# One V projection by halves of the tokens, two steps ahead of the gate transposes, and four row sums by matmul against ones

## The chip, the cores and the metric

The kernel runs on one core of a Trainium2 chip. The metric is the device time of one execution in microseconds; the median of three runs stands for a kernel. TensorE (PE, with its weight loads PEld), VectorE (DVE), ScalarE (ACT), GpSimd (POOL) and SyncE (SP, which issues almost all DMA transfers) each work through their own list of instructions in order, and wait for one another by semaphores.

## The reference

The reference is one decoder layer for 512 tokens of width 1024, in float32. The parts that matter here:

```python
mods = (silu(c) @ w_ada + b_ada).reshape(B, 9, 1, 1024)
sh1, sc1, gt1, sh2, sc2, gt2, sh3, sc3, gt3 = [mods[:, i] for i in range(9)]
h = rmsnorm(x, g_pre[0]) * (1 + sc1) + sh1
x = x + 0.5 * gt1 * rmsnorm(swiglu(h, w_gu1, w_dn1), g_post[0])      # first FFN
h = rmsnorm(x, g_pre[1]) * (1 + sc2) + sh2
y = token_mixer(h, ...)                        # z = h @ w_in, linear attention + softmax attention
x = x + gt2 * rmsnorm(y, g_post[1])
...                                            # second FFN, like the first
```

`swiglu` is 1024 to 2 x 2816, silu(g) * u, and back to 1024 through `w_dn`. In the mixer the softmax attention has 16 heads; its v is 1024 columns of `h @ w_in`, and its forget gates are 16 columns whose logarithms are summed along the tokens.

## The kernel before

Every float32 operand of a large matmul is split into a high part (fp32r) and a rest, and a product takes three matmuls (`mm3`, L203). A weight block of 128 x 1024 values is loaded by SP into one of four `raw` tiles (L151), copied to `whi` by ACT (L166), and `wlo = raw - whi` is made by DVE (L167). There are five `whi` and five `wlo` tiles. A `raw` tile is free for the next load when DVE has made its `wlo`.

The first FFN ends with `down`: two halves of the output columns (`dh`), and in each half 11 groups of two k-blocks of `w_dn` (the last three of the second half are taken together); a group is 24 matmuls, four token tiles with six each. The FFN's matmuls before that (L394 for the ordinary blocks) end with block `jb = 10`, whose results DVE multiplies (L523) and splits (L210).

Between the groups of the first half the modulation columns of the layer are made. `ada_acc` (L222, L224) loads `w_ada` in four pieces into `raw` tiles and sums, on DVE, eight rows weighted by silu(c) into one tile of 128 x 512. What is still to be summed over the 128 partitions is done on PE. For the gates (`mod_gate`) that tile is split in two (`two_parts`: ACT L209, DVE L210) and PE multiplies it with a tile of ones (L307, L308). For shift and scale of the second sub-layer (`mod_cols`, four calls, one for each 256 columns) `mod_reduce` makes four matmuls with one column of ones (L279), and `mod_turn` (L286 to L288) adds biases on DVE. The first call stands at `jb = 10`, the other three in `down`, each with its loads and sums ahead of a group and its matmuls (`rest`) behind the next one.

After `down`, `make_h` normalises and transposes x for token tiles 0 and 1, then 2 and 3 (L343, L353, L367), and the mixer begins. `Fill` is a list of steps, each with a load and a run; loads go up to four steps ahead of runs. `F.nat` adds the eight steps of one V projection: for each of four pairs of k-blocks (`kb`), first token tiles 0 and 1 (`tp = 0`), then 2 and 3. The forget gates come after the first V projection: a matmul (L787), a chain on DVE and ACT, a scan (L840), and four small transposes (L847), which wait for the scan. The steps of the second V projection are called after these in the program. The order of instructions on each engine is set by a scheduler when the kernel is built, and is fixed from then on; where several things are ready by its reckoning it does not keep to the order in which the code names them.

Of the kernel before, what the change touches and what calls it, by code (L numbers as in the profile page):

```python
# [13 lines left out]
ALU = mybir.AluOpType  # L14

P = 128
# [7 lines left out]
QA, KA, VA, AL, RA, QB, KB, VB, FB, GA, GB = (  # L24
    0, 512, 1024, 2048, 2064, 3088, 4112, 5136, 6160, 6176, 7200)
# [15 lines left out]
def tile_hybrid_layer(  # L41
# [4 lines left out]
    nc = tc.nc  # L46
# [12 lines left out]
    def nm(s):  # L59
        uid[0] += 1  # L60
        return f"{s}_{uid[0]}"

    def unit(dt=F32, shape=(P, 512)):
        return sb.tile(list(shape), dt, tag="u", bufs=NU, name=nm("u"))

    def tmp(shape=(P, 512), dt=F32):
        return sb.tile(list(shape), dt, tag="t2", bufs=NTMP, name=nm("t2"))
# [4 lines left out]
    def acc(shape=(P, 512)):  # L72
        return pm.tile(list(shape), F32, tag="mm", name=nm("mm"))

    def aux(shape=(P, 512)):
        return pa.tile(list(shape), F32, tag="aux", name=nm("aux"))

    def small(n, tag="sm", bufs=16):
        return sb.tile([P, n], F32, tag=tag, bufs=bufs, name=nm(tag))
# [25 lines left out]
    ident = sb.tile([P, P], F32, tag="ident", name="ident")  # L105
    make_identity(nc, ident)
    ones_r = sb.tile([P, P], F32R, tag="ones", name="ones")
# [93 lines left out]
    def mm3(ps, a, b, first, last):  # L201
        for n, (i, j) in enumerate(PARTS):
            nc.tensor.matmul(ps, a[i], b[j], start=first and n == 0, stop=last and n == 2)  # L203

    def cut(pair, cs):
        return pair[0][:, cs], pair[1][:, cs]

    def hilo(hi, lo, src, eng=None):
        nc.scalar.copy(hi, src)  # L209
        (eng or nc.vector).tensor_tensor(lo, src, hi.bitcast(F32), ALU.subtract)  # L210


    def ada_acc(src):

        a = tmp()
        for kh in range(4):
            raw = sb.tile([P, 2, 512], F32, tag="raw", bufs=NRAW, name=nm("raw"))
            src(raw, kh)
            for j in range(2):
                k = kh * 2 + j  # L220
                if k == 0:
                    nc.vector.tensor_scalar(a, raw[:, j, :], csil[:, 0:1], None, ALU.mult)  # L222
                else:
                    nc.vector.scalar_tensor_tensor(a, raw[:, j, :], csil[:, k:k + 1], a, ALU.mult, ALU.add)  # L224
        return a

    def two_parts(a):
        pair = unit(F32R), unit(F32R)
        hilo(*pair, a)
        return pair  # L230
# [18 lines left out]
    def ada_sum_b(us, k0):  # L249

        a = tmp()
        nc.vector.tensor_scalar(a, us[k0], csil[:, k0:k0 + 1], None, ALU.mult)
        for k in range(k0 + 1, KD):
            nc.vector.scalar_tensor_tensor(a, us[k], csil[:, k:k + 1], a, ALU.mult, ALU.add)
        nc.vector.tensor_tensor(a, a, us[0], ALU.add)
        return a

    def col_pair():
        return (sb.tile([P, KD], F32, tag="shc", bufs=2, name=nm("shc")),
                sb.tile([P, KD], F32, tag="scc", bufs=2, name=nm("scc")))  # L260

    def mod_cols(shc, scc, i, ch):

        w2 = w_ada[:, 3 * i * D:(3 * i + 2) * D].rearrange("(k p) (m c) -> p k m c", p=P, m=2)

        def src(raw, kh):
            for m in range(2):
                nc.sync.dma_start(raw[:, :, m * 256:(m + 1) * 256],
                                  w2[:, 2 * kh:2 * kh + 2, m, ch * 256:(ch + 1) * 256])
        a = ada_acc(src)  # L270

        def rest():
            mod_turn(shc, scc, i, ch, mod_reduce(a))
        return rest

    def mod_reduce(a):
        ps = aux((P, 4))
        for j in range(4):
            nc.tensor.matmul(ps[:, j:j + 1], a[:, j * P:(j + 1) * P], ones[:, 0:1], start=True, stop=True)  # L279
        return ps  # L280

    def mod_turn(shc, scc, i, ch, ps):
        js = slice(2 * ch, 2 * ch + 2)
        b0 = 24 * i + 2 * ch
        g0 = 72 + 8 * i + 2 * ch
        nc.vector.scalar_tensor_tensor(scc[:, js], ps[:, 2:4], 1.0, cols[:, b0 + 8:b0 + 10], ALU.add, ALU.add)  # L286
        nc.vector.tensor_tensor(shc[:, js], ps[:, 0:2], cols[:, b0:b0 + 2], ALU.add)
        nc.vector.tensor_tensor(scc[:, js], scc[:, js], cols[:, g0:g0 + 2], ALU.mult)  # L288
# [282 lines left out]
    with in_order(last):  # L571
# [51 lines left out]
        a = ada_sum_b(ada[0], ROWS_A[0])  # L623
# [3 lines left out]
        for ch in range(4):  # L627
            ks, part = (2 * ch, 2 * ch + 1), 3 if ch < 3 else 4
            gu_matmuls(ps0, *first, hs, ks, slice(0, 512), range(part), True)
            if ch < 3:  # L630
                a = ada_sum_b(ada[ch + 1], ROWS_A[ch + 1])
# [3 lines left out]
                modulated(ch + 1, a, (5, 4, 0)[ch])  # L635
            gu_matmuls(ps0, *first, hs, ks, slice(0, 512), range(part, 4), True)
    sh2, sc2 = col_pair()
    extra = [lambda ch=ch: mod_cols(sh2, sc2, 1, ch) for ch in range(4)]
    nxt = []

    def after1(t):
# [12 lines left out]

    sh3, sc3 = col_pair()
    extra = [lambda ch=ch: mod_cols(sh3, sc3, 2, ch) for ch in range(4)]

    halves = (slice(0, 64), slice(64, P))

    class Fill:  # L660
# [23 lines left out]
            late = []  # L684
            self.add(lambda: late.append(fn()), lambda: late[0]())

        def nat(self, c0, evac):

            blk = Block(w_in, 0, KD, c0, 512)
            ps = []  # L690

            def step(kb, tp):
                if not ps:
                    ps.extend(acc() for _ in range(NT))
                for t in (2 * tp, 2 * tp + 1):
                    for k in (2 * kb, 2 * kb + 1):
                        mm3(ps[t], cut(hs[k], slice(t * P, (t + 1) * P)), blk[k], k == 0, k == KD - 1)
                    if kb == 3:
                        evac(t, ps[t])
            for kb in range(4):  # L700
                for tp in range(2):
                    self.add(lambda kb=kb, tp=tp: None if tp else blk.load(2 * kb, 2 * kb + 2),
                             lambda kb=kb, tp=tp: step(kb, tp))

        def tr(self, todo, evac):

# [58 lines left out]
    F = Fill()  # L765
# [2 lines left out]

    vb = [[unit(), unit()] for _ in range(NT)]
    for g in range(2):  # L770
        F.nat(VB + g * 512, lambda t, ps, g=g: nc.scalar.copy(vb[t][g], ps))
    fqk = []
    F.qk_parts(QB, KB, 0.125, fqk)
    F.until(8)
# [67 lines left out]
            0.0 if i == 0 else Fr[f_, i * P - 1:i * P], ALU.mult, ALU.add)  # L842
    Fd = dr.tile([16, T], F32, name="Fd")
    nc.sync.dma_start(Fd, Fr[f_])
    ftp = aux((P, 4, 16))
    for i in range(NT):
        nc.tensor.transpose(ftp[:, i, :], Fr[f_, i * P:(i + 1) * P], ident[f_, f_])  # L847
# [167 lines left out]
    for h in range(4):  # L1015
        zp = acc()
        nc.tensor.matmul(zp, wa2[0:80, h * P:(h + 1) * P], alow[0:80], start=True, stop=True)
        u = unit()
# [272 lines left out]
```

## Time and profile before

| | |
|---|---|
| median of three runs | 1421.57 us (1421.54 to 1423.88) |
| the profiled execution | 1425.45 us, span of the profile 1423.4 us |
| PE busy | 1361.4 us, 96% of the span |
| DVE, ACT, POOL busy | 910.4, 595.5, 206.6 us |
| mean granted TensorE clock | 0.992 |

All times in the rows are microseconds from the start of the span. The profiled execution is 2.05 us longer than its span, and 3.9 us longer than the median of the three runs. PE busy counts pipelined matmuls whose ends are modelled; the step from one start to the next is the better price of a matmul.

### The profile page before, as it was taken

Reading aid. Unit: us, or ns where it says so; the run is one execution under the profiler, and the core shown is the slowest. Engines: PE = TensorE matmul, PEld = TensorE weight load, DVE = VectorE, ACT = ScalarE, POOL = GpSimd, SP = SyncE. Lnnn points to the kernel's source line nnn. Section 1 sums busy time; section 2 is a strip of 40 time slices with the busy share of each in tenths; the row PEclk is TensorE's granted clock in tenths of the full one; section 3 lists DMA queues with packets and bytes.
Section 4 is the critical chain, followed back from the end, with each engine's and each line's share of the span. In section 5 each row is a group of like instructions: output and inputs, shape, how many; then the busy total and the mean of one; then the engine's idle time right before and its main releaser. Section 6 shows DMA issues by size and latency. Waiting matters only on the chain.

```text
span 1423.4 us, 19497 instructions
## 1 busy us (share of the span) xinstructions
PE 1361.4 (96%) x7485; PEld 1146.4 (81%) x7485; DVE 910.4 (64%) x1410; ACT 595.5 (42%) x1026; POOL 206.6 (15%) x328
## 2 busy tenths in 40 slices
PE   4899999999999999999999999999999999999998
PEld 3699899888877867777888887787878999987886
DVE  6888678685266689762745546538577877866222
ACT  6444444223154476663723333332355444433221
POOL 6200000000050644340110202100050000000001
PEclk8999999999999999999999999999999999999999
DMA  9413233597336755322232232125631332346431
GB/s 322 150 62 112 82 104 110 179 290 265 103 107 182 226 163 167 94 71 78 90 117 75 60 87 62 60 74 160 210 119 45 119 119 75 104 134 196 130 118 59
DMA packets 164089, 180.84 MB, mean 127 GB/s; under 512 B 9226, under 2 KB 128118, under 8 KB 163996
## 3 DMA queue, kind: packets, MB, share of 16 engines
q1 hardware_dynamic: 163564, 178.81, 40.2%
q8 instruction: 59, 0.97, 0.3%
q10 hardware_dynamic: 432, 0.79, 0.2%
q14 instruction: 34, 0.28, 0.1%
HBM read 173.25 MB, written 6.32 MB: 126 GB/s over the span
## 4 chain that ended last, share of the span: by engine, by line
PE 71%; DVE 15%; DMA 6%; ACT 3%; issue 3%; POOL 2%; SPq 0%; DVEq 0%; POOLq 0%; ACTq 0%
PE mm L203 47%; PE mm L394 11%; PE mm L456 7%; DVE wlo L167 5%; DMA raw<-in_w_gu_dram 3%; PE aux L1108 1%; DMA u<-in_w_ada_dram 1%; DVE u L210 1%; DVE t L473 1%; ACT whi L166 1%; DMA raw<-in_w_ada_dram 1%; PE aux L919 1%; PE mm L930 1%; DVE u L907 1%; DVE raw L444 1%
## 5 line engine op out<-in xcount | busy, mean ns | idle before, releaser
L166 ACT CAST whi<-raw 128x1024 fp32r<-128x1024 f32 x262 | 273.3, 1050 | 516.7 <-PE mm L203 261.8
L167 DVE TENSOR_TENSOR wlo<-raw,whi 128x1024 fp32r<-128x1024 f32 x260 | 323.1, 1248 | 247.6 <-ACT whi L166 244.1
L203 PE MATMUL mm<-whi,u 128*128 128x512 f32 x1216 | 392.1, 398 | 1.7 <-DVE t L367 1.5
L203 PE MATMUL mm<-u,whi 128*128 128x512 f32 x896 | 289.9, 402 | 0.8 <-DVE u L1135 0.8
L456 PE MATMUL mm<-u,whi 128*128 128x256 f32 x1568 | 279.3, 281 | 10.6 <-DVE t L473 10.6
L203 PEld LDWEIGHTS mm<-whi,u 128*128 128x128 f32 x1216 | 228.2, 188 | 54.9 <-ACT u L209 1.7
L456 PEld LDWEIGHTS mm<-u,whi 128*128 128x128 f32 x1568 | 239.8, 188 | 13.9 <-DVE t L473 13.2
L203 PE MATMUL mm<-wlo,u 128*128 128x512 f32 x608 | 240.3, 395 | 1.0 <-DVE wlo L167 1.0
L456 PE MATMUL mm<-u,wlo 128*128 128x256 f32 x784 | 219.0, 280 | 0.0
L203 PEld LDWEIGHTS mm<-u,whi 128*128 128x128 f32 x896 | 167.3, 189 | 39.3 <-DVE u L1135 1.2
L394 PE MATMUL mm<-u,whi 128*128 128x512 f32 (+1 forms) x576 | 168.5, 380 | 11.0 <-ACT u L209 9.9
L203 PE MATMUL mm<-u,wlo 128*128 128x512 f32 x448 | 178.6, 399 | 0.0
L456 PEld LDWEIGHTS mm<-u,wlo 128*128 128x128 f32 x784 | 147.3, 188 | 0.0
L203 PEld LDWEIGHTS mm<-wlo,u 128*128 128x128 f32 x608 | 114.2, 188 | 28.8 <-DVE wlo L167 1.3
L394 PEld LDWEIGHTS mm<-u,whi 128*128 128x128 f32 x576 | 105.4, 191 | 35.1 <-ACT u L209 13.2
L394 PE MATMUL mm<-u,wlo 128*128 128x512 f32 (+1 forms) x288 | 105.4, 375 | 0.0
L203 PEld LDWEIGHTS mm<-u,wlo 128*128 128x128 f32 x448 | 84.7, 189 | 19.7
L321 POOL TENSOR_SCALAR sm<-ss 128x1 f32<-128x1 f32 x12 | 2.3, 190 | 642.9 <-ACT jk L328 642.9
L224 DVE SCALAR_TENSOR_TENSOR t<-raw,csil,t 128x512 f32<-128x512 f32 x98 | 74.0, 756 | 10.0 <-DMA raw<-in_w_ada_dram 7.8
L394 PEld LDWEIGHTS mm<-u,wlo 128*128 128x128 f32 x288 | 55.3, 192 | 10.3
L209 ACT CAST u<-t 128x256 fp32r<-128x256 f32 (+1 forms) x94 | 40.8, 454 | 43.5 <-DVE t L523 23.0
L876 POOL TENSOR_SCALAR u<-t,Ft 128x128 f32<-128x128 f32 (+1 forms) x64 | 44.3, 702 | 90.5 <-DMA t<-Fd 67.1
(197 smaller groups left out, 1381.1 us busy)
## 6 DMA issues: line engine op xcount, KB each, us to landing
raw<-in_w_gu_dram SPq DMA_DIRECT2D x88, 512.0 KB, 3.9
raw<-in_w_in_dram SPq DMA_DIRECT2D x64, 512.0 KB, 3.8
raw<-in_w_dn_dram SPq DMA_DIRECT2D x44, 512.0 KB, 5.2
raw<-in_w_ada_dram SPq DMA_DIRECT2D x64, 256.0 KB, 3.7
raw<-in_w_ada_dram SPq DMA_DIRECT2D x24, 512.0 KB, 5.2
u<-in_w_ada_dram SPq DMA_DIRECT2D x32, 256.0 KB, 6.3
raw<-in_w_in_dram SPq DMA_DIRECT2D x20, 256.0 KB, 2.8
t<-Fd SPq DMA_DIRECT2D x16, 256.0 KB, 5.1
```

The source lines that it names most:

```text
L166: nc.scalar.copy(hi, raw)
L167: (eng or nc.vector).tensor_tensor(lo, raw, hi.bitcast(F32), ALU.subtract)
L203: nc.tensor.matmul(ps, a[i], b[j], start=first and n == 0, stop=last and n == 2)
L209: nc.scalar.copy(hi, src)
L210: (eng or nc.vector).tensor_tensor(lo, src, hi.bitcast(F32), ALU.subtract)
L224: nc.vector.scalar_tensor_tensor(a, raw[:, j, :], csil[:, k:k + 1], a, ALU.mult, ALU.add)
L394: nc.tensor.matmul(p_[:, ts], w_[k][i][:, cs], hs[k][e][:, ts], start=ks[0] == 0 and n == 0, stop=ks[-1] == KD - 1 and n == 3 * len(ks) - 1)
L444: nc.vector.tensor_tensor(a12, a12, a11, ALU.subtract)
L456: nc.tensor.matmul(ps[:, j], *((h_[:, js], w_) if self.turned else (w_[:, js], h_)), start=first and k + j + m == 0, stop=k == 3 and m == ...
L473: nc.vector.tensor_tensor(o, ps, a, ALU.add)
L876: nc.gpsimd.tensor_scalar(s_at(s, i), fb[:, 0:n], -1.0, Ft[:, i, h:h + 1], ALU.mult, ALU.add)
L907: nc.vector.tensor_scalar(s_at(S[e], i), s_at(S[e], i), rs[e][:, i:i + 1], None, ALU.mult)
```

## The change

`mod_cols` gets a second form (`as_row`), used for the four calls of the second sub-layer: the sum tile is split in two right after it is made, PE multiplies both parts with the tile of ones (two matmuls of 128 x 512 in place of the four with one column), and DVE takes the needed column from each 128 x 128 piece by a multiplication with the identity and a sum along the row (`tensor_tensor_reduce`, four of them). The first V projection takes all four `kb` for `tp = 0` and then all four for `tp = 1`. Two steps of the list are run in front of the four gate transposes.

```diff
-    def mod_cols(shc, scc, i, ch):
+    def mod_cols(shc, scc, i, ch, as_row=False):
...
         a = ada_acc(src)
 
+        if not as_row:
+            return lambda: mod_turn(shc, scc, i, ch, mod_reduce(a))
+        hi, lo = two_parts(a)
+
         def rest():
-            mod_turn(shc, scc, i, ch, mod_reduce(a))
+
+            ps = aux()
+            nc.tensor.matmul(ps, ones_r, hi, start=True, stop=False)
+            nc.tensor.matmul(ps, ones_r, lo, start=False, stop=True)
+            own, col = tmp((P, P)), small(4)
+            for j in range(4):
+                nc.vector.tensor_tensor_reduce(own, ps[:, j * P:(j + 1) * P], ident, 1.0, 0.0,
+                                               ALU.mult, ALU.add, col[:, j:j + 1])
+            mod_turn(shc, scc, i, ch, col)
         return rest
...
-    extra = [lambda ch=ch: mod_cols(sh2, sc2, 1, ch) for ch in range(4)]
+    extra = [lambda ch=ch: mod_cols(sh2, sc2, 1, ch, True) for ch in range(4)]
...
-            for kb in range(4):
-                for tp in range(2):
-                    self.add(lambda kb=kb, tp=tp: None if tp else blk.load(2 * kb, 2 * kb + 2),
-                             lambda kb=kb, tp=tp: step(kb, tp))
+
+            for kb, tp in sorted(((kb, tp) for kb in range(4) for tp in range(2)), key=lambda u: u[1] * by_half):
+                self.add(lambda kb=kb, tp=tp: None if tp else blk.load(2 * kb, 2 * kb + 2),
+                         lambda kb=kb, tp=tp: step(kb, tp))
...
-        F.nat(VB + g * 512, lambda t, ps, g=g: nc.scalar.copy(vb[t][g], ps))
+        F.nat(VB + g * 512, lambda t, ps, g=g: nc.scalar.copy(vb[t][g], ps), g == 0)
...
     nc.sync.dma_start(Fd, Fr[f_])
+    F.run(2)
     ftp = aux((P, 4, 16))
```

The order of instructions changes with it. On DVE, at the end of block `jb = 10` and the first row sum, before the change (`t_424` is the sum tile of the first call, `t_434` and `t_437` are results of block 10, `t_453` is the sum tile of the first gate, `raw_2807` is the second group of `w_dn`, `raw_2762` the first piece of `w_ada` for the gate; `aux_2721` is what PE made of `t_424`):

```order
L167 TENSOR_TENSOR wlo_2754<-raw_2751,whi_2753 128x1024
L523 TENSOR_TENSOR t_434_2729<-t_434_2729,mm_2622 128x512
L210 TENSOR_TENSOR u_2733<-t_434_2729,u_2732 128x512
L222 TENSOR_SCALAR t_453_2761<-raw_2762,csil 128x512
L224 SCALAR_TENSOR_TENSOR t_453_2761<-raw_2762,csil,t_453_2761 128x512
L224 SCALAR_TENSOR_TENSOR t_453_2761<-raw_2766,csil,t_453_2761 128x512 x2
L523 TENSOR_TENSOR t_437_2736<-t_437_2736,mm_2624 128x512
L286 SCALAR_TENSOR_TENSOR scc_551<-aux_2721,cols 128x2
...
L224 SCALAR_TENSOR_TENSOR t_453_2761<-raw_2770,csil,t_453_2761 128x512
L167 TENSOR_TENSOR wlo_2810<-raw_2807,whi_2809 128x1024
```

The same place on DVE after the change (`aux_2725` is what PE makes of the two parts, `t_438` and `t_441` are the results of block 10, `t_457` is the gate's sum, `raw_2770` its first piece and `raw_2815` the second group of `w_dn`; L283 is the row sum, L535 the multiplication that was L523):

```order
L167 TENSOR_TENSOR wlo_2762<-raw_2759,whi_2761 128x1024
L210 TENSOR_TENSOR u_2622<-t_424_2600,u_2621 128x512
L283 ISA t_436_2728,sm_2729<-aux_2725,ident 128x128
...
L535 TENSOR_TENSOR t_438_2737<-t_438_2737,mm_2626 128x512
...
L535 TENSOR_TENSOR t_441_2744<-t_441_2744,mm_2628 128x512
...
L300 TENSOR_TENSOR scc_551<-scc_551,cols 128x2
L222 TENSOR_SCALAR t_457_2769<-raw_2770,csil 128x512
L224 SCALAR_TENSOR_TENSOR t_457_2769<-raw_2770,csil,t_457_2769 128x512
...
L167 TENSOR_TENSOR wlo_2818<-raw_2815,whi_2817 128x1024
```

The first row sum now stands ahead of both multiplications of block 10 and ahead of the gate's sums, which stood ahead of the shift and scale before. The matmuls that it reads stand on PE behind the last matmul of block 10, before and after.

On DVE at the second row sum, before the change (`t_495` is the sum tile of the third call, `aux_3012` PE's result for the second, `wlo_3074` belongs to the eighth group):

```order
L167 TENSOR_TENSOR wlo_3023<-raw_3020,whi_3022 128x1024
L222 TENSOR_SCALAR t_495_3026<-raw_3027,csil 128x512
L224 SCALAR_TENSOR_TENSOR t_495_3026<-raw_3027,csil,t_495_3026 128x512
L224 SCALAR_TENSOR_TENSOR t_495_3026<-raw_3032,csil,t_495_3026 128x512 x2
L224 SCALAR_TENSOR_TENSOR t_495_3026<-raw_3037,csil,t_495_3026 128x512 x2
L224 SCALAR_TENSOR_TENSOR t_495_3026<-raw_3042,csil,t_495_3026 128x512 x2
L286 SCALAR_TENSOR_TENSOR scc_551<-aux_3012,cols 128x2
L287 TENSOR_TENSOR shc_550<-aux_3012,cols 128x2
L288 TENSOR_TENSOR scc_551<-scc_551,cols 128x2
L167 TENSOR_TENSOR wlo_3074<-raw_3071,whi_3073 128x1024
```

And after it (`t_503` is the sum tile of the third call, `wlo_3094` belongs to the eighth group):

```order
L167 TENSOR_TENSOR wlo_3039<-raw_3036,whi_3038 128x1024
L283 ISA t_498_3027,sm_3028<-aux_3024,ident 128x128
L283 ISA sm_3028 128x1
L222 TENSOR_SCALAR t_503_3042<-raw_3043,csil 128x512
L283 ISA t_498_3027,sm_3028<-aux_3024,ident 128x128
L283 ISA sm_3028 128x1
L224 SCALAR_TENSOR_TENSOR t_503_3042<-raw_3043,csil,t_503_3042 128x512
...
L224 SCALAR_TENSOR_TENSOR t_503_3042<-raw_3058,csil,t_503_3042 128x512 x2
L167 TENSOR_TENSOR wlo_3094<-raw_3091,whi_3093 128x1024
```

The first read of PE's result moved from behind the eight sums of the third call to ahead of them; the third row sum stands in the same way ahead of the sums of the fourth call.

On PE in the first V projection, before the change (`mm_3850`, `mm_3852` are token tiles 0 and 2, `whi_3880` is `kb = 3`, `whi_3834` is `kb = 0`, `aux_3796` and `aux_3808` are the last transposes of x):

```order
L203 MATMUL mm_3850<-whi_3880,u_3619 128x512
L353 MATMUL aux_3796<-ident,t_639_3755 128x128
...
L203 MATMUL mm_3852<-whi_3834,u_3606 128x512
L203 MATMUL mm_3852<-wlo_3835,u_3606 128x512
L203 MATMUL mm_3852<-whi_3834,u_3607 128x512
L353 MATMUL aux_3808<-ident,t_639_3755 128x128
```

And after it (`mm_3888` is token tile 0, `whi_3884` is `kb = 3`):

```order
L203 MATMUL mm_3888<-whi_3884,u_3651 128x512
L365 MATMUL aux_3828<-ident,t_655_3787 128x128
...
L203 MATMUL mm_3888<-whi_3884,u_3652 128x512
L203 MATMUL mm_3888<-wlo_3885,u_3652 128x512
L203 MATMUL mm_3888<-whi_3884,u_3653 128x512
L365 MATMUL aux_3840<-ident,t_655_3787 128x128
```

The scheduler had already put `kb` 0 to 2 of tiles 0 and 1 ahead of tiles 2 and 3; what moved are nine matmuls of `kb = 3`, and the transposes ahead of them stand where they stood. The gate transposes stand behind the first matmul of `kb = 2` of the second V projection in both kernels, so the order around them did not change.

## Rows read from the trace of the kernel before

**Rows 1.** Page, busy time of the engines, share of the span, instructions.
```profile
PE 1361.4 (96%) x7485; PEld 1146.4 (81%) x7485; DVE 910.4 (64%) x1410; ACT 595.5 (42%) x1026; POOL 206.6 (15%) x328
```

**Rows 2.** PE's waits over the span: us in total, times, longest us.
```profile
PE mm L456 <- DVE t L473: 10.6, 12, 1.9
...
PE aux L353 <- DVE t L343: 1.8, 2, 1.3
...
PE mm L203 <- DVE t L367: 1.5, 1, 1.5
...
PE aux L847 <- DVE u L840: 1.3, 1, 1.3
```

**Rows 3.** Busy us by stretch; behind them granted clock, DMA share, GB/s.
```profile
281.00:341.00 60.00, 60.00 (x272) 48.80 (x272) 46.20 (x68) 16.42 (x17) 0.00 (x0) 1.00 0.87 281
341.00:408.00 67.00, 67.00 (x289) 53.85 (x288) 22.66 (x28) 19.14 (x34) 5.75 (x16) 1.00 0.41 134
408.00:455.00 47.00, 42.84 (x198) 33.68 (x197) 33.27 (x51) 25.89 (x45) 17.56 (x26) 1.00 0.52 149
```

**Rows 4.** PE's timeline at the first call and the first gate: start, us.
```profile
280.17 0.95 PE L279 MATMUL aux<-ones,t 128*128 128x1 f32 x8
280.98 0.48 PE L203 MATMUL mm<-whi,u 128*128 128x512 f32 x1
...
292.49 0.39 PE L308 MATMUL aux<-u,ones 128*128 128x512 f32 x1
292.72 0.40 PE L203 MATMUL mm<-whi,u 128*128 128x512 f32 x1
```

**Rows 5.** DVE's timeline, 274 to 311: start, us, idle before and its releaser.
```profile
274.83 0.69 DVE L523 TENSOR_TENSOR t<-t,mm 128x512 f32<-128x512 f32 x1 [7.67 <-PE mm L394]
...
276.93 0.49 DVE L222 TENSOR_SCALAR t<-raw,csil 128x512 f32<-128x512 f32 x1
277.45 2.33 DVE L224 SCALAR_TENSOR_TENSOR t<-raw,csil,t 128x512 f32<-128x512 f32 x3
...
283.35 1.22 DVE L167 TENSOR_TENSOR wlo<-raw,whi 128x1024 fp32r<-128x1024 f32 x1
...
296.95 1.23 DVE L167 TENSOR_TENSOR wlo<-raw,whi 128x1024 fp32r<-128x1024 f32 x1
...
310.94 0.48 DVE L222 TENSOR_SCALAR t<-raw,csil 128x512 f32<-128x512 f32 x1
```

**Rows 6.** SP's queue: when `w_dn` loads of the first FFN are issued.
```profile
278.23 1.94 SPq L151 DMA_DIRECT2D raw<-in_w_dn_dram  x2
...
312.23 1.94 SPq L151 DMA_DIRECT2D raw<-in_w_dn_dram  x2
```

**Rows 7.** ACT's timeline: the copy of the eighth group's weights.
```profile
318.57 1.05 ACT L166 CAST whi<-raw 128x1024 fp32r<-128x1024 f32 x1 [8.81 <-DMA raw<-in_w_dn_dram]
```

**Rows 8.** Groups by form: busy us, mean ns of one, idle before, releasers.
```profile
L167 DVE TENSOR_TENSOR wlo<-raw,whi 128x1024 fp32r<-128x1024 f32 x260 | 323.1, 1248 | 247.6 <-ACT whi L166 244.1 <-PE aux L1143 1.6 <-DMA raw<-in_w_in_dram 1.4
L224 DVE SCALAR_TENSOR_TENSOR t<-raw,csil,t 128x512 f32<-128x512 f32 x98 | 74.0, 756 | 10.0 <-DMA raw<-in_w_ada_dram 7.8
L894 DVE DVE_READ_ACCUMULATOR2_ANT sm<- 128x1 f32 x64 | 5.2, 82 | 0.0
L894 DVE CUSTOM_DVE_ANT_0 u<-mm,u 128x128 f32<-128x128 f32 x16 | 4.5, 289 | 4.3 <-PE mm L890 3.7 <-PE mm L891 0.4
```

**Rows 9.** DMA issues: count, KB each, median us from issue to landing.
```profile
raw<-in_w_in_dram SPq DMA_DIRECT2D x64, 512.0 KB, 3.8
raw<-in_w_dn_dram SPq DMA_DIRECT2D x44, 512.0 KB, 5.2
```

**Rows 10.** Two stretches with a lower granted clock; columns as in rows 3.
```profile
20.00:31.00 11.00, 6.12 (x18) 4.83 (x19) 9.85 (x12) 7.62 (x12) 8.10 (x5) 0.53 1.10 352
...
620.20:625.00 4.80, 4.62 (x16) 3.67 (x17) 4.32 (x12) 0.77 (x1) 2.35 (x4) 0.64 0.29 95
```

**Rows 11.** PE's timeline: the wait just ahead of the second of these stretches.
```profile
620.11 0.30 PE L890 MATMUL mm<-u,u 128*128 128x128 f32 x1 [1.82 <-DVE u L758]
```

More of the change, by code (lines that the diff above doesn't have):

```diff
@@ L685, in extra, with nat @@
             self.add(lambda: late.append(fn()), lambda: late[0]())
-        def nat(self, c0, evac):
+        def nat(self, c0, evac, by_half=False):
             blk = Block(w_in, 0, KD, c0, 512)
```

## The prediction

> **What bounds the kernel now.** I read the page first: PE is busy for 1361.4 of 1423.4 us, 96% [rows 1], so time is won or lost only where PE waits or where its own work shrinks. The list of PE's waits is next: the boundary between the first FFN and the mixer holds 1.5 us for the first h (L203 <- L367), 1.3 of the 1.8 us for the normalised rows (L353 <- L343), and 1.3 us ahead of the gate transposes (L847) [rows 2]. That is 4.1 us in all, and it is what two of the three edits can reach. The third edit lies earlier. The stretch table shows it: from 281 to 341 us PE is busy for all of 60 us, but DVE for 46.2, and the DMA engines for 0.87 of it at 281 GB/s; from 341 to 408 PE is again full [rows 3]. So the first half of `down` runs with full PE on supplies that come only just in time. The last view is DVE's timeline there. The second group's `wlo` starts at 283.35 and is done at 284.6; PE gets to it at 280.98 + 24 x 0.23 = 286.6. The fourth group's is done at 298.18, and PE needs it at 292.72 + 25 x 0.23 = 298.5: 0.3 us in hand [rows 4, 5].
>
> **Row sums: what PE saves.** The four one-column matmuls take PE from 280.17 to 280.98, 0.81 us; two of 128 x 512 take 2 x 0.23 = 0.47, by the step from 292.49 to 292.72 [rows 4]. That is 0.35 us a call, 1.4 us for four.
>
> **Row sums: what DVE and ACT get.** For each call one copy on ACT and one subtraction on DVE of 128 x 512 (0.69 us, the size of the L523 row [rows 5]), and four row sums. The trace has no such sum, but the same custom form with 128 x 128 from PSUM at L894: 289 + 82 ns for reading the accumulator [rows 8], 0.37 us each, 1.5 us a call. I take this; its bounds are 0.29 and 0.45. If DVE were free, 60 - 46.2 = 13.8 us of idle time would cover all 8.8 us. It isn't the amount that costs but the place.
>
> **The first call.** In the order after the change the first row sum is ahead of both multiplications of block 10 and of the gate's sums. It reads what PE makes behind the last matmul of that block, so DVE stands still until 280.17 + 0.23 + 0.39 = 280.8. Before, DVE took up that work at 274.83, did the gate's first sums at 276.93 and 277.45 [rows 5], and with the first piece of `w_ada` used up SP could issue the second group's load at 278.23 [rows 6]. Queued behind the row sum now: four sums (1.5), two multiplications and two subtractions (4 x 0.69 = 2.8), three small operations (0.4), then L222 and one L224 (0.51 + 0.76) until that `raw` tile is free: 280.8 + 6.0 = 286.8. The load is 8.6 us late. It lands after 3.8 us (the `w_in` median) to 5.2 us (the `w_dn` median) [rows 9]; I take 4.5, since little else is in flight: 291.3. ACT's copy takes 1.05 [rows 7] and DVE, which has by then done the other six sums (6 x 0.76), 1.25: `whi` 292.3, `wlo` 293.6. PE comes to it at 280.64 + 24 x 0.23 = 286.2, waits 6.1 us, does three matmuls, and waits 0.6 more: 6.7 us, bounds 6.0 and 7.4. The fourth group had 0.3 us in hand. Its load is late by the same 8.6 us less the pauses that DVE had in between, 1.6 us, and PE by 6.7 - 0.35; so a further 0 to 1.8 us, and I take 0.5, near the lower end, because fewer loads compete now.
>
> **The second and third call.** Here the row sum moved ahead of eight sums of the next call. Count from t, the start of the second matmul with ones. DVE can read at t + 0.4, and frees the first piece after two row sums, L222 and L224: t + 2.4. Before, DVE began these sums at 310.94, without waiting for PE, and the load was issued at 312.23 [rows 5, 6]. Landing after 4.5: t + 6.9, `whi` t + 8.0; DVE's remaining six sums, two row sums and small operations end at t + 8.2, `wlo` t + 9.4. PE comes to `whi` after 24 matmuls, t + 5.8, waits 2.2, does four matmuls and one with ones, and waits again: 9.4 - (5.8 + 5 x 0.23) = 2.4 us in all. If the load took 6.3 us, as the one from 312.23 to its copy at 318.57 did [rows 6, 7], it would be 4.0; if DVE's instructions overlap more than I count, 1.5. Two calls: 4.8 us, bounds 3.0 and 8.0. The fourth call's sums stand behind `wlo` tiles of the second half of `down`, more than a group ahead of PE, where DVE has 44 us of 67 free [rows 3]: nothing, and 1 us if that cover is gone.
>
> **The clock.** After the wait of 1.82 us at 620.11 the granted clock fell to 1.2 GHz (0.64 in the mean from 620.20 to 625.00) [rows 10, 11], which cost 4.8 x 0.36 = 1.7 us. From 20 to 31 us, among long waits at the start, it was 0.53: 11 x 0.47 = 5.2 us. The boundary's waits of 1.3 to 1.5 us, and those of up to 1.9 at L456 [rows 2], cost no clock (1.00 from 408 to 455 [rows 3]). A wait of 6 us should drop it once: I take 1.7, since the work around it is as dense as at 620, and nothing for the later two.
>
> The Trainium skill, "TensorE: Matmul & The Clock Gate", section "HAM oscillation", describes a kernel whose clock fell at every wait for a load, with half of each throttled time as the price. By that rule all three waits drop the clock, and the sum would be 1.7 us larger for each of the other two. This trace agrees at 620.11, and not at the waits at L456.
>
> **The V projection and the gate transposes.** The scheduler had `kb` 0 to 2 of tiles 0 and 1 in front already. Nine matmuls of `kb = 3` move, but the transposes that end each wait stand where they stood, and what PE does between them was never waiting for the later halves. The four weight pairs are held some 13 matmuls, 3 us, longer; the second projection is over 10 us away. The gate transposes stay behind the same matmul, so their 1.3 us stay. Both edits: 0; bounds -1.5 (the waits shorten, if copies of V come earlier) and +0.6 (one 0.6 us copy on ACT ahead of the last casts of h, if its cover, DVE's pause, is gone).
>
> **Sum.** -1.4 + 6.7 + 0.5 + 4.8 + 1.7 = +12.3 us. Nothing gives it back: from 341 to 408 PE is full. On the profiled execution's 1425.45 us (span 1423.4 and 2.05 around it) that is 1437.8; on the median of the runs, which is 3.9 us lower, 1421.57 + 12.3 = 1433.9.
>
> **Rivals.**
> - *The edits do what they say.* PE loses 1.4 us of work and the 4.1 us of boundary waits: 1416. It decides if the second group's load is issued before about 280, so that `wlo` is there at 286.2. Against it: DVE works in order, and the piece that must be freed is read behind the row sum. For it: DVE's idle 7.67 us before 274.83 [rows 5]. A chance of 0.03.
> - *The holds are hidden.* All of DVE's delay is taken up by weights already there: within 0.2% of 1421.6. Only the first group is there, 5.6 us of work. 0.05.
> - *Only the first call costs.* PE's lateness lets the loads run ahead, so the later two find their pieces free: -1.4 + 6.7 + 0.5 + 0 to 1.7 = 1427 to 1429. Against it: their row sums wait for PE itself, however late PE is. 0.17.
> - *The clock falls at each wait, or longer at the first.* With the price of the start (5.2) or three times 1.7: 1437 to 1441. 0.2.
>
> **Numbers.** The forecast, three waits and one drop, has a chance of 0.55, and by its own bounds lies from 1430 to 1437. Eight in ten have to reach over the two slower and milder cases: 1427 to 1441. 0.2% is 2.8 us, about what a measurement of this kernel can tell from no change; slower by more 0.92, within it 0.05, faster 0.03.
>
> **What would show it.** In the profile after: DVE idle from about 268 until 280.8, with the row sum's line and PE as releaser; SP's second `w_dn` load near 287; PE waits of 5 to 7 us at L203 near 286 for ACT's `whi`, and two of 1.5 to 3 us further on; a lower granted clock behind the first; the waits at L353 and at the transposes unchanged. I am wrong if the load is issued before 281, if PE stays full from 281 to 341, or if the boundary's waits vanish.

## The result and the profile after

The changed kernel takes 1431.42 us (median of four runs, 1429.5 to 1435.19) against 1421.71 us for the kernel before on the same chip (1421.54 to 1423.88): a ratio of 1.0067, 95% interval 1.0053 to 1.0081, so 9.5 us slower, between 7.5 and 11.5. The forecast was +12.3 us, range 1427 to 1441.

The profiled execution took 1430.82 us, span 1429.1. The list of PE's waits over the span (total, times, longest) answers to [rows 2]:

```profile
PE mm L203 <- ACT whi L166: 5.6, 3, 4.0
...
PE aux L365 <- DVE t L355: 1.8, 2, 1.3
...
PE mm L203 <- DVE t L379: 1.5, 1, 1.5
...
PE aux L860 <- DVE u L852: 1.3, 1, 1.3
PE mm L203 <- DVE wlo L167: 1.2, 2, 0.7
```

The three waits at the boundary are what they were, to a tenth: 1.8, 1.5 and 1.3 us (L353, L367 and L847 are L365, L379 and L860 now). What is new is the first line: 5.6 us of waiting for `whi`, where before that pair stood at 0.2. The stretches say where; columns as in [rows 3]:

```profile
281.00:341.00 60.00, 53.67 (x218) 41.09 (x217) 46.37 (x82) 12.33 (x14) 0.00 (x0) 0.97 0.76 237
341.00:408.00 67.00, 67.00 (x289) 53.91 (x288) 24.64 (x35) 20.93 (x33) 3.72 (x9) 1.00 0.53 170
```

PE was busy for all 60 us of the first stretch; now it is for 53.67. The first call in DVE's timeline, to be held against [rows 5]:

```profile
277.66 0.29 DVE L283 CUSTOM_DVE_ANT_0 t<-aux,ident 128x128 f32<-128x128 f32 x1 [13.08 <-PE aux L280]
...
281.25 0.48 DVE L222 TENSOR_SCALAR t<-raw,csil 128x512 f32<-128x512 f32 x1
281.76 5.47 DVE L224 SCALAR_TENSOR_TENSOR t<-raw,csil,t 128x512 f32<-128x512 f32 x7
287.23 1.22 DVE L167 TENSOR_TENSOR wlo<-raw,whi 128x1024 fp32r<-128x1024 f32 x1
```

SP's issues of the `w_dn` loads behind the holds:

```profile
282.54 1.95 SPq L151 DMA_DIRECT2D raw<-in_w_dn_dram  x2
...
321.32 2.19 SPq L151 DMA_DIRECT2D raw<-in_w_dn_dram  x2
...
334.25 9.62 SPq L151 DMA_DIRECT2D raw<-in_w_dn_dram  x6
```

ACT's copies of what those loads brought, the second and the eighth group:

```profile
286.15 1.04 ACT L166 CAST whi<-raw 128x1024 fp32r<-128x1024 f32 x1 [5.72 <-DMA raw<-in_w_dn_dram]
...
325.00 1.05 ACT L166 CAST whi<-raw 128x1024 fp32r<-128x1024 f32 x1 [10.89 <-DMA raw<-in_w_dn_dram]
```

And PE's timeline: the first matmul with ones, and its four waits in this half of `down`, at the second, sixth, eighth and tenth group:

```profile
276.99 0.40 PE L279 MATMUL aux<-u,ones 128*128 128x512 f32 x1
...
287.25 1.65 PE L203 MATMUL mm<-whi,u 128*128 128x512 f32 x3 [4.01 <-ACT whi L166]
...
313.59 0.51 PE L203 MATMUL mm<-wlo,u 128*128 128x512 f32 x1 [0.74 <-DVE wlo L167]
...
326.10 1.19 PE L203 MATMUL mm<-whi,u 128*128 128x512 f32 x4 [0.81 <-ACT whi L166]
...
338.98 1.20 PE L203 MATMUL mm<-whi,u 128*128 128x512 f32 x4 [0.77 <-ACT whi L166]
```

DVE stands still for 13 us until PE has made the first row sum's operand, frees the gate's first piece only then, the load leaves at 282.54, and PE stops from 283.24 to 287.25. Behind that stop the clock is lower (stretches, columns as before):

```profile
281.00:284.00 3.00, 2.23 (x10) 1.48 (x8) 2.89 (x6) 0.00 (x0) 0.00 (x0) 1.00 0.11 14
284.00:288.00 4.00, 0.75 (x2) 0.66 (x3) 3.86 (x6) 1.04 (x1) 0.00 (x0) 0.91 0.81 251
288.00:292.00 4.00, 4.00 (x14) 3.02 (x13) 2.23 (x4) 1.57 (x2) 0.00 (x0) 0.66 0.97 335
292.00:296.00 4.00, 4.00 (x19) 3.22 (x18) 3.86 (x7) 0.00 (x0) 0.00 (x0) 1.00 0.90 285
```

The spans differ by 5.7 us only. The reason is that the two executions had come apart by 3.2 us before the first of these instructions: PE's first column matmul started at 280.17 before [rows 4], its first matmul with ones at 276.99 after. Over all the profiled executions below that start lies between 276.99 and 280.17, also where nothing ahead of it differs. So each kernel is read over one segment too: from that start to the mixer's first matmul on the new h, which is 410.43 before and 415.09 after:

```profile
410.43 0.50 PE L203 MATMUL mm<-whi,u 128*128 128x512 f32 x1 [1.46 <-DVE t L367]
```

```profile
415.09 0.50 PE L203 MATMUL mm<-whi,u 128*128 128x512 f32 x1 [1.46 <-DVE t L379]
```

| kernel | time, us (median) | ratio to before, 95% interval | segment in the profile, us |
|---|---|---|---|
| before | 1421.7 to 1423.6 in four sets of runs | | 130.26 |
| changed | 1431.42 | 1.0067 (1.0053 to 1.0081) | 138.10 |
| V projection and gate transposes only | 1424.53 | 1.0006 (0.9994 to 1.0018) | 131.42 |
| row sums only | 1431.77 | 1.0055 (1.0039 to 1.0071) | 138.63 |
| hold only | 1430.27 | 1.0048 (1.0034 to 1.0061) | 138.51 |
| row form, first call | 1430.52 | 1.0050 (1.0038 to 1.0063) | 136.30 |
| row form, later three | 1425.50 | 1.0018 (1.0008 to 1.0029) | 131.65 |
| filled | 1429.95 | 1.0051 (1.0037 to 1.0065) | 137.26 |
| piece first | 1427.79 | 1.0037 (1.0021 to 1.0052) | 135.05 |
| late reads | 1422.51 | 0.9996 (0.9986 to 1.0007) | 128.56 |
| late reads, row sums only | 1422.79 | 0.9997 (0.9986 to 1.0008) | 128.58 |
| late reads, pinned, steps early | 1428.50 | 1.0041 (1.0028 to 1.0054) | 128.57 |
| late reads, pinned | 1423.41 | 1.0003 (0.9991 to 1.0015) | 128.56 |

Over the segment the change costs 7.84 us, inside the interval of the runs. A segment is read from one execution of each kernel, the ratios from all runs.

### The profile page after: what moved, and what is told of

Same layout as the page of the kernel before. It is cut to its first block, busy times and chain, and to the rows that moved or that the text cites. A ratio compares the mean times of both kernels' runs of the same rounds, so it can differ in the third digit from the quotient of the medians.

```text
span 1429.1 us, 19493 instructions
## 1 busy us (share of the span) xinstructions
PE 1364.9 (96%) x7461; PEld 1146.7 (80%) x7461; DVE 916.1 (64%) x1446; ACT 597.6 (42%) x1030; POOL 207.8 (15%) x328
## 4 chain that ended last, share of the span: by engine, by line
PE 68%; DVE 17%; DMA 7%; ACT 3%; issue 3%; POOL 1%; DVEq 0%; SPq 0%; POOLq 0%; ACTq 0%
PE mm L203 44%; PE mm L406 11%; PE mm L468 7%; DVE wlo L167 5%; DMA raw<-in_w_gu_dram 3%; DMA raw<-in_w_dn_dram 2%; DVE u L210 1%; PE aux L1121 1%; ACT whi L166 1%; DVE t L485 1%; DMA u<-in_w_ada_dram 1%; DVE t L224 1%; PE aux L932 1%; PE mm L943 1%; DVE raw L450 1%
```

## The experiments

**Which edit.** Two kernels, each the changed kernel with a part taken back; the row form is off in the first:

```diff
-    extra = [lambda ch=ch: mod_cols(sh2, sc2, 1, ch, True) for ch in range(4)]
+    extra = [lambda ch=ch: mod_cols(sh2, sc2, 1, ch) for ch in range(4)]
```

> The changed kernel with the row sums of the second sub-layer in the old form; the first V projection by halves and the two steps ahead of the gate transposes stay. My theory (both edits hardly move an instruction on PE, and the waits at the boundary do not depend on them): within 1.5 us of the kernel before, 1420 to 1423 where that is at 1421.7; the waits at the h tile, the normalised rows and the gate transposes stay at 1.5, 1.3 and 1.3 us. The rival that the boundary takes part of the loss: 1424 or more, with longer waits between 405 and 460 us. The rival that the two edits do what they say: 1418 to 1420, with the boundary's waits shorter.

and, with the row form on,

```diff
-        F.nat(VB + g * 512, lambda t, ps, g=g: nc.scalar.copy(vb[t][g], ps), g == 0)
+        F.nat(VB + g * 512, lambda t, ps, g=g: nc.scalar.copy(vb[t][g], ps))
...
-    F.run(2)
     ftp = aux((P, 4, 16))
```

> The row sums for the four calls of the second sub-layer alone; V projection and gate transposes as before. My theory (all of the loss comes from here): as the changed kernel, 1429.5 to 1433, about 9.7 us over the kernel before, with one PE wait of about 4 us at the second group of the first half of down, three of 0.7 to 0.9 later, and one drop of the clock. The rival that it takes all three edits: 1426 or less.

The first is 0.06% slower, interval -0.06 to +0.18%: no difference that shows. The second carries the loss, +7.8 us (5.5 to 10.1), in the segment +8.4 against the +7.8 of the whole change. In the first kernel's profile the boundary's waits are 1.5 (h) and 1.7 us (transposes), not shorter. One row of it matters for later:

```profile
309.62 0.50 PE L203 MATMUL mm<-wlo,u 128*128 128x512 f32 x1 [0.77 <-DVE wlo L167]
```

The sixth group waits 0.77 us for its `wlo` here too, in a kernel without row sums, and the profile of the row sums alone has no wait there. So the 0.74 us at 313.59 above can't be put down to the row sums. That profile has the long wait (4.37 us) and then two, of 1.00 and 1.10 us, where three of 0.7 to 0.9 were expected.

**Place or work.** The kernel before, with nothing added, only DVE's order pinned (`after_inst(i, j)` keeps `i` behind `j` on their engine):

```diff
             mod_turn(shc, scc, i, ch, mod_reduce(a))
+            if i == 1 and ch < 3:
+                turned.append(list(nc.cur_bb.bb.instructions)[-1])
...
                     nc.vector.tensor_scalar(a, raw[:, j, :], csil[:, 0:1], None, ALU.mult)
+                    if turned:
+                        after_inst(list(nc.cur_bb.bb.instructions)[-1], turned.pop())
...
                 nc.vector.tensor_tensor(th, th, pu, ALU.mult)
+                if turned:
+                    after_inst(list(nc.cur_bb.bb.instructions)[-1], turned[-1])
```

> The kernel before, with its old one-column sums, and only DVE's order changed: the shift and scale of each call are held ahead of what comes next on DVE (for the first call ahead of the multiplications of block 10 and the gate's sums, for the second and third ahead of the next call's sums), where the row sums stand in the changed kernel. It has none of the extra work on DVE, ACT and PE. My theory (the place costs, not the work): DVE stands still until about 281, SP's second load of w_dn leaves 6 us later than before, PE waits about 3.5 us for it, the clock drops once, and three waits of up to 1 us follow: 1427.5 to 1432. The rival that the added work (9 us on DVE, 2.5 on ACT) is what delays the weights: within 1.5 us of the kernel before.

Its DVE waits, then its PE:

```profile
279.69 0.16 DVE L292 SCALAR_TENSOR_TENSOR scc<-aux,cols 128x2 f32<-128x2 f32 x1 [14.00 <-PE aux L285]
```

```profile
288.57 1.65 PE L203 MATMUL mm<-whi,u 128*128 128x512 f32 x3 [3.21 <-ACT whi L166]
```

+6.8 us (4.8 to 8.7) without one added instruction, in the segment +8.25: the place costs, also without the work. Behind the hold, work adds to the price: the wait here is 3.21 us, the changed kernel's 4.01. The reverse keeps all the work and moves the reads of the first three calls behind the next call's sums:

```diff
+        last_sum = list(nc.cur_bb.bb.instructions)[-1]
+        while pend:
+            start = len(nc.cur_bb.bb.instructions)
+            pend.pop(0)()
+            for i in list(nc.cur_bb.bb.instructions)[start:]:
+                after_inst(i, last_sum)
         return a
...
-            mod_turn(shc, scc, i, ch, col)
+            if ch < 3:
+                pend.append(read)      # read(): the four row sums and mod_turn
+            else:
+                read()
```

> The changed kernel with all its operations, but DVE reads the row sums of the first three calls behind the last of the next call's eight sums instead of ahead of them. PE's order, and all work on every engine, stay as in the changed kernel. My theory (only the place of the reads costs): the loads of w_dn leave as early as before the change, the PE waits of 4.0, 0.7, 0.8 and 0.8 us in the first half of down and the drop of the clock there are gone, and the 1.4 us that PE saves remain: 1419 to 1421.5, 10 to 12 us under the changed kernel. The rival that the row sums' own work or their later results cost: 1424 or more.

Its stretch, against the same of the changed kernel above:

```profile
281.00:341.00 60.00, 60.00 (x258) 48.23 (x257) 51.67 (x101) 17.38 (x20) 0.00 (x0) 1.00 0.87 283
```

PE is full again, while DVE does 51.67 us of work in place of 46.20. The segment is 1.70 us shorter than before, the time 0.04% lower, interval -0.14 to +0.07%. So the row sums' own work is free there. The forecast gain over the kernel before shows in the segment alone; the runs do not resolve it.

**Which call.** The row form for `ch == 0` alone, and for `ch > 0` alone:

```diff
-    extra = [lambda ch=ch: mod_cols(sh2, sc2, 1, ch, True) for ch in range(4)]
+    extra = [lambda ch=ch: mod_cols(sh2, sc2, 1, ch, ch == 0) for ch in range(4)]
```

> The changed kernel with the row form for the first of the four calls alone; the other three take the old one-column sums. My theory (three separate holds; the first carries the one long wait and the clock): PE waits about 4 us at the second group, the clock drops there for 1.7 to 3.4 us in price, no waits of 0.7 us or more at the eighth and tenth group: 5 to 8 us over the kernel before. The rival that the later calls cost as much as the first: 4 us or less over it.

> The changed kernel with the row form for the second, third and fourth call, the old sums for the first. My theory: no long wait near 286 and no drop of the clock there, waits of 0.8 to 1.1 us at the eighth and the tenth group, 1 us of PE work saved: 0.5 to 2.5 us over the kernel before. As forecast (two waits of 2.4 us): 3.7 us over it. The rival that the later holds are free: 1 us under it.

PE in the first kernel, and in the second:

```profile
289.38 1.65 PE L203 MATMUL mm<-whi,u 128*128 128x512 f32 x3 [4.07 <-ACT whi L166]
```

```profile
322.81 1.20 PE L203 MATMUL mm<-whi,u 128*128 128x512 f32 x4 [1.07 <-ACT whi L166]
...
335.56 1.20 PE L203 MATMUL mm<-whi,u 128*128 128x512 f32 x4 [0.73 <-ACT whi L166]
```

Segments +6.0 and +1.4; times +7.1 us (5.4 to 9.0) and +2.6 us (1.1 to 4.1). The first hold costs most, the later two are small but there: "free" falls. The 3.7 us of the forecast lie inside the interval of the runs; against them speak the two waits, 1.07 and 0.73 us where 2.4 each were forecast, and the segment.

**The load or DVE's queue.** The prediction let the late load decide. Here, starting from the late reads, the first call's reads (`reads`) and block 10's multiplications (`mults`) stand behind the two sums that use the first piece, so the piece is free before the hold; the other six of the eight `sums` stay behind it. The row sums also write their products over PE's result instead of into a tile of their own.

```diff
-                after_inst(i, last_sum)
+                after_inst(i, sums[1 if mults else -1])
+            for i in mults + sums[2:] if mults else ():
+                after_inst(i, reads[0])
```

> The kernel with the late reads, but the first call's row sum goes back ahead of block 10's multiplications and of six of the gate's eight sums; only the two sums that read the first piece stay ahead of it, so that this piece is free, and the second group's load of w_dn leaves, before DVE's hold begins. (The row sums write their products back over PE's result instead of into a tile of their own.) If the load alone carries the first call's cost: the load leaves near 276, whi is there long before PE, no wait near 286, and the time is that of the late reads, within 1.5 us of the kernel before. If DVE's queue carries it as well (wlo is made behind all that the hold delays, about 11 us after PE's first matmul with ones, and PE wants it 6.5 us after that): whi comes in time, but PE waits about 4.5 us for wlo, the clock drops, and the time is 4.5 to 7 us over the kernel before.

SP, DVE, ACT and PE:

```profile
266.22 0.37 SPq L151 DMA_DIRECT2D raw<-in_w_dn_dram  x1
```

```profile
277.95 0.30 DVE L297 CUSTOM_DVE_ANT_0 aux<-aux,ident 128x128 f32<-128x128 f32 x1 [11.76 <-PE aux L292]
...
285.99 1.20 DVE L167 TENSOR_TENSOR wlo<-raw,whi 128x1024 fp32r<-128x1024 f32 x1
```

```profile
286.61 1.04 ACT L166 CAST whi<-raw 128x1024 fp32r<-128x1024 f32 x1 [5.62 <-DMA raw<-in_w_dn_dram]
287.56 0.61 ACT L209 CAST u<-t 128x512 fp32r<-128x512 f32 x1
```

```profile
288.22 0.80 PE L337 MATMUL aux<-u,ones 128*128 128x512 f32 x1 [3.78 <-ACT u L209]
```

The load leaves at 266.22, 16 us earlier than in the changed kernel, and PE still stops for 3.78 us, from 284.4: `wlo` stands in DVE's queue until 287.2, and the gate's own split until 288.2, for which PE has a matmul with ones in front. The last 1.0 us of this is ACT's queue: the split stands there behind the copy of the third group's weights, which waits for their load until 286.61. Without that PE would have stopped until `wlo` at 287.2 all the same. The time is +5.3 us (3.0 to 7.4). So the early load alone doesn't help.

**The clock.** The changed kernel with 14 matmuls that nothing reads, pinned to the place where PE would stop:

```diff
+FILL = 14
...
+                if dh == 0 and k0 == 2 and len(extra) == 3:
+                    fill = aux()
+                    for _ in range(FILL):
+                        nc.tensor.matmul(fill, ones_r, act[0][0], start=True, stop=True)
+                        after_inst(list(nc.cur_bb.bb.instructions)[-1], pe_last)
+                        pe_last = list(nc.cur_bb.bb.instructions)[-1]
...
                 for t in range(NT):
```

> The changed kernel with 14 idle matmuls of 128 x 512 (3.3 us, into a tile that nothing reads) put on PE just ahead of the second group, where it waits 4 us for weights. My theory (the wait has a second price, the lower clock behind it): the granted clock stays at 2.4 GHz through this stretch, PE's wait there shrinks to about 0.7 us plus up to 1 us for the rest that comes late, and the time is 0.7 to 3.4 us under the changed kernel's 1431.5: 1428 to 1431. The rival that the drop of the clock costs nothing of its own, since the weights behind it are as late: the same as the changed kernel.

Its stretch (the changed kernel's clock there: 0.66), and PE (this kernel's lines are one further on):

```profile
288.00:292.00 4.00, 3.94 (x18) 2.88 (x17) 3.03 (x4) 1.57 (x2) 0.00 (x0) 1.00 0.95 314
```

```profile
287.56 1.20 PE L204 MATMUL mm<-whi,u 128*128 128x512 f32 x4 [0.83 <-ACT whi L167]
...
299.43 1.02 PE L204 MATMUL mm<-whi,u 128*128 128x512 f32 x2
301.21 0.50 PE L204 MATMUL mm<-wlo,u 128*128 128x512 f32 x1 [0.76 <-DVE wlo L168]
```

The clock stays up, and the segment is only 0.84 us shorter than the changed kernel's, not 1.7. The wait of 0.76 us at 301.21, at the fourth group, is new, but the changed kernel's 0.74 us at the sixth is gone in turn. With the 3.2 us of the 14 matmuls PE's idle time is 6.5 us in all, against 6.3. The other 0.7 us is in steps that are longer beside the late weights though no wait is listed: two matmuls from 299.43 take 1.02 us, where 0.63 is usual, and four from 287.56 take 1.26 to the next one, where 0.93 is usual. The times (1.0051 and 1.0067) don't tell the two kernels apart; that half of the price is lost again in this way rests on one profile each.

**Faster than both?** The late reads without the other two edits, and then with the gate transposes held behind 11 more matmuls. This is done in two ways: by running five steps of the list early (on top of all three edits; the diff), or by the pin alone, set when the matmuls it waits for are written. The kernel with the early steps also runs five in place of two ahead of the four heads of the linear attention, later in the mixer:

```diff
-    F.run(2)
+    F.run(5)
+    pe_last = [i for i in nc.cur_bb.bb.instructions if i.engine == mybir.EngineType.PE][-1]
...
         nc.tensor.transpose(ftp[:, i, :], Fr[f_, i * P:(i + 1) * P], ident[f_, f_])
+        after_inst(list(nc.cur_bb.bb.instructions)[-1], pe_last)
...
     hd.prep()
-    F.run(2)
+    F.run(5)
```

> The row form with the late reads, V projection and gate transposes as in the kernel before. My theory: 1.4 us of PE work saved in the first half of down and nothing else: 0.5 to 2 us under the kernel before. The rival that the two other edits give something that the late reads' run had: no gain here.

> The kernel with the late reads, and the gate transposes held on PE behind the first two token tiles of the third pair of k-blocks of the second V projection (11 matmuls, 2.6 us, more work ahead of them), so that the order around them does change. My theory (what the edit ahead of the transposes meant to reach is the wait of 1.3 us, and only the order decides): the wait is gone, also the drop of the clock behind it that the late reads' profile had, and the time is 1 to 3 us under the kernel with the late reads: 1.5 to 4 us under the kernel before. The rival that the transposes' later end delays the attention scores: no gain.

> The same, with the gate transposes held on PE behind the first two token tiles of the third pair of k-blocks of the second V projection, this time without running any step of the list earlier, so that the rest of the mixer keeps its order. My theory: the wait of 1.3 to 1.9 us at the transposes goes, with the drop of the clock that follows it in some executions: 1 to 3 us under the row form with late reads alone, 2 to 4.5 us under the kernel before, the fastest of all. The rival that the later transposes delay the attention scores as much: no gain over it.

Both theories on the transposes fall. Their first wait goes, and two others come, at the third and the fourth transpose, each for its part of the scan; behind them the clock is 0.57 from 455 to 459. With the pin alone:

```profile
453.55 0.23 PE L878 MATMUL aux<-ident,u 16*128 16x16 f32 x1 [1.06 <-DVE u L871]
...
455.31 0.28 PE L878 MATMUL aux<-ident,u 16*128 16x16 f32 x1 [0.63 <-DVE u L871]
```

The kernel with the early steps is 5.8 us (4.0 to 7.7) slower than the kernel before, but not through the transposes. The same two instructions of PE, with the pin alone and then with the early steps, are 0.1 us apart behind the transposes and 4.6 us apart at the end of the heads:

```profile
618.38 0.30 PE L922 MATMUL mm<-u,u 128*128 128x128 f32 x1 [1.87 <-DVE u L788]
...
959.39 0.68 PE L1175 MATMUL aux<-ident,u 128*128 128x128 f32 x4 [0.99 <-DVE u L1168]
```

```profile
618.27 0.30 PE L919 MATMUL mm<-u,u 128*128 128x128 f32 x1 [1.87 <-DVE u L784]
...
949.79 1.88 PE L1137 MATMUL aux<-u 128*126 128x64 f32 x16
953.93 3.92 PE L203 MATMUL mm<-u,u 128*128 128x256 f32 x18 [2.26 <-ACT u L209]
...
964.00 0.68 PE L1172 MATMUL aux<-ident,u 128*128 128x128 f32 x4 [0.99 <-DVE u L1165]
```

So it is the five steps ahead of the heads that cost: at 949.79 two rounds of small matmuls stand without a step between them, and a wait of 2.26 us follows, with a drop of the clock behind it (0.89 from 950 to 965). No other kernel has that wait. No run took the two places apart; this rests on the two profiles. The pin alone gives 1.0003 (0.9991 to 1.0015). The late reads alone give 0.9997 (0.9986 to 1.0008), which neither shows nor excludes the 0.5 to 2 us expected of them. No version measurably beats the kernel before; the 1.7 us saved in the segment is below what the runs resolve.

## Why the prediction was right, point by point

- **The place of the first row sum**: right, and shown twice, by the hold alone and by the late reads. Its size was too large: 6.7 us, bounds 6.0 to 7.4, against a wait of 4.0, which lies outside these bounds. Counted from PE's first matmul with ones, the load left after 5.55 us, not 6.6, since DVE's instructions overlap by some 0.1 us each (L535 steps by 0.60 with 0.68 of duration). It was at ACT 3.6 us after its issue (282.54 to 286.15), not 4.5. These two make 2.0 of the 2.1 us. The further 0.6 us for `wlo` didn't come, because PE was at half clock by then.
- **The load as the cause** was half of it. With the load 16 us earlier PE still stops for 3.78 us, of which DVE's queue, by its `wlo` at 287.2, makes some 2.7. In the changed kernel both were late: `whi` was ready at 287.19, and DVE reached `wlo` at 287.23. There is no run with a late load and a free DVE queue; that the load alone would do it is worked out and not shown.
- **The second and third call**: 4.8 us, bounds 3.0 to 8.0; measured 0.81 and 0.77 us of idle time, outside these bounds. By the segment of the later three, +1.4 us with three savings of 0.42 each (below) inside, they cost some 2.6 together: after such a wait PE's first steps are longer too (0.34 us from 313.59 to the next matmul, where others take 0.23). Counted from t, the start of the second matmul with ones (319.29), the row sum began at t + 0.43 and the load left at t + 2.03, against 0.4 and 2.4 in the forecast. The term that was most off is again the landing, 3.7 us (321.32 to 325.00) in place of 4.5; with the earlier start of the load that is 1.2 of the 1.6 us a call.
- **The fourth group**, +0.5: no wait is listed, only two steps of 0.34 us at 300.58 and 300.92. The one at the sixth group (0.74) also stands in a kernel without row sums.
- **The clock**, 1.7 for one drop: 0.66 over 4 us and 0.91 over 4 is 1.7 us in the profile, and the waits of 0.7 to 0.8 cost none (the stretch from 299 to 341 had 1.00). That the size agrees to the tenth is luck: in the profile of the row sums alone, where PE does the same matmuls in the same order, the drop cost some 2.8 us (last section). The clock fell at the first of the four waits for weights alone. The Trainium skill, "TensorE: Matmul & The Clock Gate", section "HAM oscillation", tells of a kernel whose waits for loads took some 3 to 5 us and whose clock fell at each. The first wait here, 4.0 us, agrees with that; the two later waits of the forecast, 2.4 us, and those measured, 0.7 to 0.8, are shorter than any in that section, so the prediction read it too widely when it let them drop the clock by it. Worth 1.7 on paper, the drop was worth half of that where it could be taken away.
- **What PE saves**: 1.4 forecast, 1.70, 1.68, 1.69 and 1.70 us in the four segments with late reads, 0.42 a call. The columns cost 0.81 us, and the first matmul behind them stepped by 0.31 (279.52 to 279.83 in the hold kernel) where 0.23 is usual; that last part was missing.
- **V projection and gate transposes**, 0: right within the interval, for the reason given (the order around the waits didn't change).
- **The rivals.** "Only the first call costs" gave 1427 to 1429, which is 5.8 to 7.5 us over the kernel before. The first call alone does cost 7.1, but the later two add 2.6 (1.1 to 4.1) to it, so it falls. "Hidden" and "as they say" fall with the 4.0 us wait. "The clock falls at each wait" falls with the 1.00 from 299 to 341; its other half, a longer drop at the first, shows in the profile of the row sums alone, at some 2.8 us and not 5.2.

Altogether the segment's +7.84 is -1.7 saved, 4.0 and 2.3 us of idle time, 1.7 of clock, and 1.5 that is left over. What is left over is the part of the waits that their idle time leaves out. It counts from the modelled end of the matmul before, 0.40 us after that one's start, where the next usually starts after 0.23: 0.17 for each of four waits, 0.7 us. And nine steps at the three later waits and at the fourth group take 0.31 to 0.36 us in place of 0.23, 1.0 us more. The forecast of +12.3 was 4.5 too high: 2.7 in the first hold, 3.2 in the idle time of the later calls, 0.5 for the fourth group and 0.3 in the saving, less 0.7 at the sixth group and that 1.5. So the path was right (a row sum that is read too early, a load that leaves late, PE without weights), and the sizes of both waits were not. That the time came out inside 1430 to 1437 all the same is in part luck: 2.2 us of it (0.7 and 1.5) are costs that the sum did not have.

## What to carry to other kernels

An instruction on an in-order engine costs what stands behind it while it waits, not its own duration: 7.4 us of added work on DVE (917.8 us busy with the late reads, 910.4 before) were free, and three tiny reads of a matmul's result, placed ahead of sums that could have run, cost 8 us in the segment (6.8 in the runs). When a change makes an engine read another's result, look where the scheduler put that read, and pin it behind the work that is ready. A wait placed between other waits moves rather than goes: filler for one gap is taken from another (the steps run ahead of the heads were missing at the last of them), and clock won back is partly lost beside weights that are still late.

## What the runs showed of the hardware

The same wait doesn't always bring the lower clock. At the gate transposes PE waited 1.86 us in the late reads' profile and 1.75 us in that of the V projection edits; just behind, the granted clock was 0.53 in the one and 1.00 in the other:

```profile
454.30:457.70 3.40, 3.40 (x9) 2.27 (x9) 2.38 (x4) 0.00 (x0) 0.00 (x0) 0.53 0.57 159
```

```profile
454.20:457.60 3.40, 3.40 (x14) 2.33 (x15) 3.27 (x5) 0.07 (x1) 0.00 (x0) 1.00 0.42 102
```

Nor does the drop last the same. Behind the hold kernel's wait of 3.21 us, shorter than the changed kernel's 4.01, the clock was 0.58 over 8 us, which is 6.7 us at 1.2 GHz. PE still waited for the first 0.57 us; half of the rest is the price, 3.1 us. In the profile of the row sums alone, behind a wait of 4.37 us, it was 0.57 over the same 8 us, of which PE waited for 1.27: some 2.8 us. The hold kernel, then the row sums alone:

```profile
288.00:296.00 8.00, 7.43 (x20) 5.85 (x21) 6.67 (x10) 2.19 (x3) 0.00 (x0) 0.58 0.88 293
```

```profile
288.00:296.00 8.00, 6.73 (x18) 5.17 (x19) 6.64 (x10) 2.61 (x3) 0.00 (x0) 0.57 0.96 312
```

What decides this stays open. Whether it is part of why medians of the kernel before lay 2 us apart between sets of runs is not shown.
